# Sums over keys of the stick-breaking heads as products with the high and the low part of the softplus, and rotation of q and k with priority on VectorE

## The chip, the cores and the metric

The kernel runs on one core of one Trainium2 chip. The metric is the device time of one execution in microseconds (us). TensorE multiplies matrices into PSUM, VectorE and ScalarE work element by element, GpSimd does small work beside them, and SyncE issues most DMA transfers.

## The reference

Two blocks follow each other, for 256 positions of width 1024, all in float32. The first block has two layers; its first layer is the one that matters here. Its attention has 16 heads of 64 values each: eight stick-breaking heads and eight block-attention heads whose q and k are rotated by position first.

```
z   = q k^T / 8                                  (stick-breaking heads)
log_1mb = where(key < query, log_sigmoid(-z), 0)
after   = reverse cumulative sum over keys of log_1mb, without the key itself
a   = where(key < query, exp(log_sigmoid(z) + after), 0);   out = a v
q, k of the other eight heads: [x1 cos - x2 sin, x2 cos + x1 sin], then a causal softmax
```

Then come the projection of all heads, the gated feed-forward layers, a retention layer, and the second block of two layers.

## The kernel before

The kernel is one straight program. Weights are streamed from HBM as 1 MB tiles `raw`. ScalarE casts each to a high part `whi` (line 350, type float32r, which TensorE multiplies in one pass) and VectorE subtracts that to get a low part `wlo` (line 351). A product of two float32 matrices is then three float32r products: high by high, high by low, low by high (`mm3`; below, one group is these three products of 512 columns). Plain float32 operands are multiplied too, in two instructions each in the trace. Small float32 products and all transposes go that way.

TensorE's order is the order in which the Python program emits its instructions. A virtual clock `now` grows by a given cost per product (the last but two arguments of `mm`), and jobs (Python generators) are put into a heap with due times. Whenever a group is emitted, jobs that are due emit their part: `yield 9.42` (`D_SB`) means that the job goes on 9.42 virtual microseconds later. The orders of the other engines are written by a scheduler at build time, by a priority that is the program's order. `with self.first():` raises the priority of the instructions in it by 250 places. All orders are fixed when the kernel runs: an engine waits in its queue for whatever its next instruction needs.

In the first layer, after the first projection, each of the eight stick-breaking heads is one job (`sb_job`, line 649). Its first part multiplies k by q into a PSUM bank (256 + 128 columns; two 128-wide key blocks, the second one meeting only the second half of the queries). ScalarE then makes `e` = ln(1 + exp(-|z|)) in three passes (lines 663 to 665), and VectorE makes `sp` = max(z, 0) + e, the softplus, and masks it (lines 666, 668). Its second part, due 9.42 later, adds the sums over keys to the same bank as products of `sp` with the constant matrices `ntri` (minus one on and below the diagonal) and `nones` (all minus one), both kept in the tile `sq`. These are three float32 products of 256, 128 and 128 columns. ScalarE takes the exponential into `aT` (line 673), and VectorE masks it (line 674). `e` has three buffers (tag "sbe") and `sp` three (tag "sm").

Beside these jobs runs the projection of q and k of the other eight heads (`gemm_col`, blocks b = 1 for q, b = 2 for k, each for two halves t of the positions, eight groups each). When a half is done, its job (`epi`, line 857) rotates it on VectorE in four instructions (`rotary`, lines 616 to 619) into a tile `rows`, and 5.49 virtual microseconds later (`D_ROT0`) TensorE transposes `rows` in four instructions (line 284, from `trs`) and ScalarE copies them to `qT` or `kT` (line 865). Rotations below are counted in this order: first and second (q), third and fourth (k). The tag "rows" has four buffers of 512 columns. Also on VectorE, in the background, run the products of a vector with weights that make the modulation rows (`acc`, line 575) of three such rows in this layer; each ends in a split (`acch` line 491, `accl` line 492) that TensorE then uses.

Of the kernel before, what the change touches and what calls it, by code (L numbers as in the profile page):

```python
# [10 lines left out]
F32 = mybir.dt.float32  # L11
F32R = mybir.dt.float32r
AF = mybir.ActivationFunctionType
ALU = mybir.AluOpType
# [232 lines left out]
class Kern:  # L247
# [407 lines left out]
    def sb_job(self, q, k, aT):  # L655
        V, A = self.V, self.A
        qT, kT = q(), k()
        ps = self.bank()
        self.mm(ps[:, 0:256], kT[:, 0:128], qT, True, True, 0.432, True)
        self.mm(ps[:, 256:384], kT[:, 128:256], qT[:, 128:256], False, True, 0.216, True)  # L660
        e = self.ph.tile([128, 384], F32, tag="sbe", bufs=3, name=self.nm("sbe"))
        sp = self.ph.tile([128, 384], F32, tag="sm", bufs=self.smb, name=self.nm("sbs"))
        A.activation(e, ps[:, :384], AF.Abs)
        A.activation(e, e, AF.Exp, scale=-1.0)
        A.activation(e, e, AF.Ln, bias=1.0)
        V.scalar_tensor_tensor(sp, ps[:, :384], 0.0, e, ALU.max, ALU.add)
        d2 = lambda x: x.rearrange("p (j n) -> p j n", n=128)[:, 0:3:2]
        V.tensor_tensor(d2(sp), d2(sp), self.strict, ALU.mult)
        yield D_SB
        self.mm(ps[:, 0:256], self.ntri, sp[:, 0:256], False, True, 0.432, True)  # L670
        self.mm(ps[:, 128:256], self.nones, sp[:, 256:384], False, True, 0.216, True)
        self.mm(ps[:, 256:384], self.ntri, sp[:, 256:384], False, True, 0.216, True)
        A.activation(aT, ps[:, :384].rearrange("p (j n) -> p j n", n=128), AF.Exp)
        V.scalar_tensor_tensor(aT[:, 0:3:2], aT[:, 0:3:2], BIG, self.strict, ALU.min, ALU.mult)
        yield 2.5


    def startup(self, p):


        nc, V, A = self.nc, self.V, self.A
# [4 lines left out]
        nc.scalar.dma_start(cc, a["c"])  # L686
        self.ident = b.tile([128, 128], F32, name="ident")
        nc.scalar.dma_start(self.ident, a["k_sq"][:, 0:128])
        sq = p.tile([128, 256], F32, name="sq")
        nc.scalar.dma_start(sq, a["k_sq"][:, 128:384])  # L690
        self.ntri, self.nones = sq[:, 0:128], sq[:, 128:256]
        self.ones = p.tile([128, 128], F32, name="ones")
        V.memset(self.ones, 1.0)
        self.ones_r = p.tile([128, 128], F32R, name="ones_r")
# [67 lines left out]
        ps = [[self.bank() for _ in range(3)] for _ in range(2)]  # L762
        lst, lsv = chunks_of(D, QKV0)[0], chunks_of(D, QKV_BLOCKS)[0]
        w = {"w": {}, "v": {}}
# [58 lines left out]
    def layer0(self, lp):  # L823
        nc, V, A = self.nc, self.V, self.A
        with self.pool("l0") as p:
# [5 lines left out]
            rope = p.tile([128, 2, 3, 32], F32, name="rope64")  # L831
# [26 lines left out]
            def epi(b, t, _, ps):  # L858
                if b == 3:
                    A.copy(v[1][:, t], ps)  # L860
                    return
                rows = self.wk.tile([128, 512], F32, tag="rows", bufs=4, name=self.nm("rows"))
                self.rotary(rows, ps, rope, t, 8, 32)
                yield D_ROT0
                A.copy((qT if b == 1 else kT)[1][:, :, t * 128:t * 128 + 128], self.trs(rows, 4))

# [22 lines left out]
            for pr in range(4):  # L889

                avj[pr] = self.spawn(av(pr, [sj[i] for i in range(8)]), 1.0)
            qkj = self.gemm_col(h, "w_qkv", ch[1:3], epi, 1)
            for hd in range(8, 16):
                sj[hd] = self.spawn(score(hd, qkj), 0.5 + (hd - 8) * SP_MB)
            vj = self.gemm_col(h, "w_qkv", ch[3:4], epi, 3)
            for pr in range(4, 8):
                avj[pr] = self.spawn(av(pr, vj + [sj[i] for i in range(8, 16)]), 1.0)
# [655 lines left out]
```

## Time and profile before

| | us |
|---|---|
| median of 3 runs | 1475.32 (1473.52 to 1475.45) |
| the profiled execution: time | 1474.96 |
| the profiled execution: span of the trace | 1473.0 |
| TensorE busy in it | 1448.8 |
| VectorE busy | 1046.3 |
| ScalarE busy | 813.6 |
| GpSimd busy | 106.4 |

The span runs from the first to the last instruction that the trace holds; the profiled execution's own time is 1.96 us longer. In the rows, PE is TensorE, PEld its weight load, DVE VectorE, ACT ScalarE, POOL GpSimd. A matmul's duration is its own from start to end and overlaps the next one's; what a product costs is read from one start to the next. An engine's idle time before an instruction stands in square brackets, with what ended it. "PEclk" is the granted clock of TensorE as a share of full speed: 1.00 is 2.4 GHz, 0.50 is 1.2 GHz.

### The profile page before, as it was taken

The numbers are of one execution on the slowest core, as the hardware profiler recorded it, in microseconds if no ns is written. First come the engines' busy times: TensorE is split into PE (matmuls) and PEld (weight loads), VectorE is DVE, ScalarE is ACT, GpSimd is POOL, SyncE is SP. The second block draws the span as 40 slices with busy tenths as digits, with TensorE's granted clock in tenths as the row PEclk, the third lists the DMA queues.
The fourth block names the chain that finished last, engine by engine and source line by source line (L and its number), as shares of the span: only waits on it lengthen the run. The fifth ranks groups of instructions, "written<-read, shape, count | busy, mean of one in ns | idle before, by whom it ended". The sixth has DMA issues, their size and how long they took to land.

```text
span 1473.0 us, 19815 instructions
## 1 busy us (share of the span) xinstructions
PE 1448.8 (98%) x7476; PEld 1185.7 (80%) x7476; DVE 1046.3 (71%) x1675; ACT 813.6 (55%) x1365; POOL 106.4 (7%) x88
## 2 busy tenths in 40 slices
PE   8999999999999999999999999999999999999998
PEld 6776788887887888888878888888888888888887
DVE  5688898956988848966378756565666866666664
ACT  4657556643544535655356755666445675566651
POOL 0000000000001000000012012110000201221000
PEclk9999999999999999999999999999999999999999
DMA  9757587765776646755435455455535545555452
GB/s 380 280 201 271 199 315 287 286 207 184 284 272 243 235 165 233 297 185 197 165 123 194 166 184 210 162 177 172 193 143 190 188 147 206 195 188 189 158 175 82
DMA packets 53091, 306.64 MB, mean 208 GB/s; under 512 B 7674, under 2 KB 12154, under 8 KB 20100
## 3 DMA queue, kind: packets, MB, share of 16 engines
q1 hardware_dynamic: 51988, 304.87, 57.8%
q8 instruction: 59, 0.97, 0.3%
q10 hardware_dynamic: 1008, 0.50, 0.1%
q14 instruction: 36, 0.29, 0.1%
HBM read 301.16 MB, written 1.05 MB: 205 GB/s over the span
## 4 chain that ended last, share of the span: by engine, by line
PE 88%; DVE 5%; ACT 2%; DMA 2%; POOL 1%; issue 1%; ACTq 0%; DVEq 0%; POOLq 0%
PE p L280 84%; PE p L284 4%; DVE wlo L351 2%; ACT whi L350 1%; DMA raw<-in_w_in_dram 1%; POOL qss L487 1%; POOL ss L519 0%; DMA as<-in_ada_s_dram 0%; DVE junk L527 0%; DMA sq<-in_k_sq_dram 0%; DVE res L554 0%; DMA raw<-in_w_ao_dram 0%; DVE acc L575 0%; DVE x L555 0%; ACT sm L636 0%
## 5 line engine op out<-in xcount | busy, mean ns | idle before, releaser
L280 PE MATMUL p<-whi,hT 128*128 128x512 f32 (+1 forms) x2240 | 748.1, 401 | 4.9 <-DVE hT L492 2.7
L351 DVE TENSOR_TENSOR wlo<-raw,whi 128x1024 fp32r<-128x1024 f32 x450 | 538.2, 1215 | 147.9 <-ACT whi L350 143.9
L350 ACT CAST whi<-raw 128x1024 fp32r<-128x1024 f32 x450 | 461.8, 1045 | 242.7 <-PE p L280 189.4
L280 PEld LDWEIGHTS p<-whi,hT 128*128 128x128 f32 x2240 | 422.8, 189 | 99.7 <-issue 7.3
L280 PE MATMUL p<-wlo,hT 128*128 128x512 f32 (+1 forms) x1120 | 437.6, 391 | 0.0
L280 PEld LDWEIGHTS p<-wlo,hT 128*128 128x128 f32 x1120 | 212.1, 189 | 39.2 <-issue 1.7
L280 PE MATMUL p<-hT,whi 128*128 128x512 f32 x576 | 199.2, 398 | 0.0
L280 PE MATMUL p<-hT,wlo 128*128 128x256 f32 x576 | 149.9, 281 | 0.0
L280 PEld LDWEIGHTS p<-hT,whi 128*128 128x128 f32 x576 | 103.8, 188 | 19.6
L280 PEld LDWEIGHTS p<-hT,wlo 128*128 128x128 f32 x576 | 108.7, 189 | 6.6
L575 DVE SCALAR_TENSOR_TENSOR acc<-raw,csc,acc 128x1024 f32<-128x1024 f32 x80 | 102.2, 1277 | 3.5 <-DMA raw<-in_ada_w_dram 3.2
L487 POOL TENSOR_TENSOR dss<-dss,mh 128x8 f32<-128x8 f32 (+3 forms) x36 | 56.1, 1557 | 318.2 <-DVE dss L486 318.2
L280 PE MATMUL p<-whi,al 128*128 128x512 f32 x176 | 69.5, 395 | 0.0
L280 PE MATMUL p<-wlo,ah 128*128 128x512 f32 x176 | 69.5, 395 | 0.0
L280 PE MATMUL p<-whi,ah 128*128 128x512 f32 x176 | 69.5, 395 | 0.0
L1410 DVE TENSOR_TENSOR rows<-p,dss 128x512 f32<-128x512 f32 (+3 forms) x36 | 18.5, 514 | 46.2 <-POOL dss L487 46.2
L962 ACT COPY fT<-p 128x256 f32<-128x256 f32 x72 | 26.2, 370 | 45.2 <-PE p L280 45.2
L519 POOL TENSOR_TENSOR ss<-ss,mh 128x1 f32<-128x1 f32 x14 | 13.4, 960 | 471.2 <-DVE ss L518 471.2
L280 PE MATMUL p<-whi,s 128*128 128x512 f32 x128 | 41.3, 397 | 0.0
L280 PEld LDWEIGHTS p<-wlo,ah 128*128 128x128 f32 x176 | 33.0, 187 | 8.1
L280 PEld LDWEIGHTS p<-whi,al 128*128 128x128 f32 x176 | 33.0, 187 | 8.0
L280 PEld LDWEIGHTS p<-whi,ah 128*128 128x128 f32 x176 | 33.0, 187 | 8.0
(262 smaller groups left out, 1621.1 us busy)
## 6 DMA issues: line engine op xcount, KB each, us to landing
raw<-in_w_in_dram SPq DMA_DIRECT2D x84, 1024.0 KB, 4.9
raw<-in_w_gu_dram SPq DMA_DIRECT2D x44, 1024.0 KB, 5.2
raw<-in_ada_w_dram SPq DMA_DIRECT2D x40, 1024.0 KB, 5.3
raw<-in_w_ret_dram SPq DMA_DIRECT2D x24, 1024.0 KB, 4.9
raw<-in_w_dn_dram SPq DMA_DIRECT2D x22, 1024.0 KB, 4.9
raw<-in_w_qkv_dram SPq DMA_DIRECT2D x11, 1024.0 KB, 5.7
as<-in_ada_s_dram SPq DMA_DIRECT2D x16, 512.0 KB, 10.0
raw<-in_w_ro_dram SPq DMA_DIRECT2D x8, 1024.0 KB, 6.1
```

Source lines behind the costliest of these rows:

```text
L280: self.T.matmul(out, lhsT=lhsT, rhs=rhs, start=first, stop=last, skip_group_check=skip)
L284: self.T.transpose(out, in_, self.ident)
L350: for ins in (self.A.copy(hi[:, :m * n], src), self.V.tensor_tensor(lo[:, :m * n], src, hi[:, :m * n].bitcast(F32), ALU.subtract)):
L351: self.V.tensor_tensor(lo[:, :m * n], src, hi[:, :m * n].bitcast(F32), ALU.subtract)):
L487: self.G.tensor_tensor(ss, ss, self.mh[:, :n], ALU.pow)
L519: self.G.tensor_tensor(ss[:, 0:1], ss[:, 0:1], self.mh[:, 0:1], ALU.pow)
L575: self.V.scalar_tensor_tensor(acc, r[:, j * D:j * D + D], self.sc[:, k:k + 1], acc, ALU.mult, ALU.add)
L962: A.copy(f, ps[:, 256:512])
L1410: V.tensor_tensor(d3(rows[:, :nu * 128]), d3(src), ss[:, :2 * nu, None].to_broadcast([128, 2 * nu, 64]), ALU.mult)
```

## The change

In the stick-breaking job, `e` and `sp` move to buffers of the tag "rows" (four, shared with the rotated tiles). Two new tiles take their old buffers: `hi`, a float32r copy of `sp` made by ScalarE, and `lo` = `sp` - `hi`, made by GpSimd. The constants are cast once, at the start, to a float32r tile `sqr` by VectorE, and the tile `sq` moves to a buffer of the tag "rtmp". The three float32 products become six float32r products, three with `hi` and three with `lo`; the virtual costs become 0.12 and 0.067. The due times 9.42 and 5.49 stay. In the job of the projection, the four rotation instructions stand inside `with self.first()`.

```diff
         ps = self.bank()
         self.mm(ps[:, 0:256], kT[:, 0:128], qT, True, True, 0.432, True)
         self.mm(ps[:, 256:384], kT[:, 128:256], qT[:, 128:256], False, True, 0.216, True)
-        e = self.ph.tile([128, 384], F32, tag="sbe", bufs=3, name=self.nm("sbe"))
-        sp = self.ph.tile([128, 384], F32, tag="sm", bufs=self.smb, name=self.nm("sbs"))
+        e, sp = (self.wk.tile([128, 512], F32, tag="rows", bufs=4, name=self.nm(n))[:, 0:384] for n in ("sbe", "sbs"))
...
         V.tensor_tensor(d2(sp), d2(sp), self.strict, ALU.mult)
+
+        hi = self.ph.tile([128, 384], F32R, tag="sbe", bufs=3, name=self.nm("sbh"))
+        lo = self.ph.tile([128, 384], F32R, tag="sm", bufs=self.smb, name=self.nm("sbl"))
+        A.copy(hi, sp)
+        self.G.tensor_tensor(lo, sp, hi.bitcast(F32), ALU.subtract)
         yield D_SB
-        self.mm(ps[:, 0:256], self.ntri, sp[:, 0:256], False, True, 0.432, True)
-        self.mm(ps[:, 128:256], self.nones, sp[:, 256:384], False, True, 0.216, True)
-        self.mm(ps[:, 256:384], self.ntri, sp[:, 256:384], False, True, 0.216, True)
+        for w in (hi, lo):
+            self.mm(ps[:, 0:256], self.ntri, w[:, 0:256], False, False, 0.12, True)
+            self.mm(ps[:, 256:384], self.ntri, w[:, 256:384], False, w is lo, 0.067, True)
+            self.mm(ps[:, 128:256], self.nones, w[:, 256:384], False, w is lo, 0.067, True)
         A.activation(aT, ps[:, :384].rearrange("p (j n) -> p j n", n=128), AF.Exp)
...
-        sq = p.tile([128, 256], F32, name="sq")
+        sq = self.wk.tile([128, 256], F32, tag="rtmp", name="sq")
         nc.scalar.dma_start(sq, a["k_sq"][:, 128:384])
-        self.ntri, self.nones = sq[:, 0:128], sq[:, 128:256]
+        sqr = p.tile([128, 256], F32R, name="sqr")
+        V.tensor_copy(sqr, sq)
+        self.ntri, self.nones = sqr[:, 0:128], sqr[:, 128:256]
...
                 rows = self.wk.tile([128, 512], F32, tag="rows", bufs=4, name=self.nm("rows"))
-                self.rotary(rows, ps, rope, t, 8, 32)
+                with self.first():
+                    self.rotary(rows, ps, rope, t, 8, 32)
                 yield D_ROT0
                 A.copy((qT if b == 1 else kT)[1][:, :, t * 128:t * 128 + 128], self.trs(rows, 4))
```

## Rows read from the trace of the kernel before

**Rows 1.** The page, part 1: engine, busy us, share of the span, instructions.
```profile
PE   1448.8 (98%) x7476; PEld 1185.7 (80%) x7476; DVE 1046.3 (71%) x1675; ACT 813.6 (55%) x1365; POOL 106.4 (7%) x88
```

**Rows 2.** Waits of PE, 0 to 200 us: us in total, times, longest.
```profile
PE p L284 <- DVE rows L619: 3.7, 2, 3.4
```

**Rows 3.** Timeline of PE, 62 to 125 us: start, us, instruction, [idle before].
```profile
77.33 0.60 PE L284 MATMUL p<-ident,rows 128*128 128x128 f32 x4
77.68 0.48 PE L280 MATMUL p<-whi,hT 128*128 128x512 f32 x1
...
79.63 2.90 PE L280 MATMUL p<-sbs,sq 128*128 128x256 f32 x18
...
84.98 1.04 PE L280 MATMUL p<-sbs,sq 128*128 128x256 f32 x6
85.78 0.48 PE L280 MATMUL p<-whi,hT 128*128 128x512 f32 x1
...
87.94 1.04 PE L280 MATMUL p<-sbs,sq 128*128 128x256 f32 x6
...
94.62 1.09 PE L284 MATMUL p<-ident,rows 128*128 128x128 f32 x4 [3.38 <-DVE rows L619]
...
99.35 1.56 PE L280 MATMUL p<-sbs,sq 128*128 128x256 f32 x6
100.66 0.47 PE L280 MATMUL p<-whi,hT 128*128 128x512 f32 x1
```

**Rows 4.** Timeline of DVE, 62 to 125 us.
```profile
79.43 0.68 DVE L616 TENSOR_TENSOR rows<-p,rope 128x512 f32<-128x512 f32 x1
80.03 1.28 DVE L575 SCALAR_TENSOR_TENSOR acc<-raw,csc,acc 128x1024 f32<-128x1024 f32 x1
81.22 1.10 DVE L666 SCALAR_TENSOR_TENSOR sbs<-p,sbe 128x384 f32<-128x384 f32 x2
...
90.74 0.42 DVE L617 TENSOR_TENSOR rt<-p,rope 128x256 f32<-128x256 f32 x1
...
93.79 0.68 DVE L619 TENSOR_TENSOR rows<-rows,rt 128x512 f32<-128x512 f32 x1
```

**Rows 5.** Stretches of 1 us: busy of PE, PEld, DVE, ACT, POOL; PEclk; DMA share; GB/s.
```profile
99.00:100.00 1.00, 1.00 (x4) 0.81 (x3) 0.97 (x3) 0.00 (x0) 0.00 (x0) 0.50 0.59 250
```

**Rows 6.** Timeline of PE, 205 to 216 us: float32r products of 256 columns.
```profile
206.15 0.40 PE L280 MATMUL p<-hT,wlo 128*128 128x256 f32 x2
206.38 0.63 PE L280 MATMUL p<-hT,whi 128*128 128x512 f32 x2
```

**Rows 7.** Instructions on the tile sbs: count, duration ns min/median/max, first and last start.
```profile
L280 PEld LDWEIGHTS p<-sbs,sq x48: 186/192/337, 79.6 to 100.5; 128*128 128x128 f32 x48
```

**Rows 8.** Instructions on the tile sbe.
```profile
L663 ACT ACTIVATE sbe<-p x8: 473/487/496, 69.3 to 83.4; 128x384 f32<-128x384 f32 x8
```

**Rows 9.** Groups of GpSimd, shapes apart: count, busy us, mean ns, idle before.
```profile
L487 POOL TENSOR_TENSOR dss<-dss,mh 128x8 f32<-128x8 f32 x12 | 25.1, 2092 | 188.6 <-DVE dss L486 188.6
L566 POOL MEMSET acc<- 128x1024 f32 x10 | 9.6, 956 | 329.0 <-DVE accl L492 218.6 <-DMA raw<-in_ada_w_dram 88.2 <-issue 21.9
```

**Rows 10.** Timeline of POOL, 155 to 170 us.
```profile
160.14 0.55 POOL L519 TENSOR_TENSOR ss<-ss,mh 128x1 f32<-128x1 f32 x1 [11.22 <-DVE ss L518]
167.14 1.46 POOL L519 TENSOR_TENSOR ss<-ss,mh 128x1 f32<-128x1 f32 x1 [6.45 <-DVE ss L518]
```

**Rows 11.** Timeline of DVE, 95 to 170 us.
```profile
98.31 0.69 DVE L616 TENSOR_TENSOR rows<-p,rope 128x512 f32<-128x512 f32 x1 [1.69 <-PE p L280]
...
101.47 0.42 DVE L674 SCALAR_TENSOR_TENSOR aT<-aT,strict 128x256 f32<-128x256 f32 x1 [1.08 <-ACT aT L673]
102.72 1.23 DVE L351 TENSOR_TENSOR wlo<-raw,whi 128x1024 fp32r<-128x1024 f32 x1 [0.83 <-ACT whi L350]
...
166.99 1.21 DVE L351 TENSOR_TENSOR wlo<-raw,whi 128x1024 fp32r<-128x1024 f32 x1
```

**Rows 12.** DMA issues: line's tiles, queue, count, KB each, us to landing.
```profile
sq<-in_k_sq_dram ACTq DMA_DIRECT2D x1, 128.0 KB, 6.6
```

## The prediction

> **What bounds the kernel now.** I read the page's shares first: TensorE is busy 1448.8 of 1473.0 us [rows 1], so a change counts if it takes time from TensorE's own work or from its waits. Next the waits of TensorE, to see where its 24 idle us lie: in the first 200 us the largest is the transposes of a rotated tile waiting for VectorE, twice, 3.7 in all, the longest 3.4 [rows 2]. TensorE's timeline places the long one: it stands idle for 3.38 before 94.62 [rows 3]. VectorE's timeline says why: the second rotation starts at 79.43, and its second instruction comes at 90.74, its last at 93.79, with `acc` and other work of earlier places in the program between them [rows 4]. The data was there; the order kept it back. Last the granted clock: at 99 to 100 it is 0.50 [rows 5], the 1.2 GHz level, after that idle stretch. So the wait is paid twice, once as idle time and once as slow products behind it.
>
> **The change part by part.** The sum is made against the profiled execution, 1474.96 us.
>
> *Rotation first.* The four instructions cost VectorE the same (0.68 + 0.42 + 0.42 + 0.68 = 2.2) [rows 4], but follow each other: 79.43 + 2.2 = 81.6, in place of about 94.4. The transposes that need them came at 91.24 in TensorE's order (94.62 less the wait). By the virtual costs in the code they also move forward: the first head's sums now advance the clock by 0.51 and not 0.86, so the projection's job is spawned before the second head's sums and not after the fourth's, and its transposes stand behind the fifth head's and not the seventh's. I put them at about 87, five us after 81.6. So the 3.38 goes, and with it the 0.3 of the fourth rotation [rows 2]: 3.7.
>
> *The clock.* From 94.62 to 100.66 TensorE took 6.04 for four transposes, nine products of 512 columns (three groups) and one head's sums [rows 3]. At full clock the same cost 0.35 (77.33 to 77.68), 2.16 (85.78 to 87.94) and 0.80 (84.98 to 85.78), in all 3.3. Without the idle stretch 2.7 goes too.
>
> *The sums as six one-pass products.* Before, at full clock: 2.9 for the first three heads and 0.80 for each of the other five [rows 3], 6.9 in all. After, each head has two products of 256 columns and four of 128. The 256 are shown: two in 0.23, or 0.12 each [rows 6]. A one-pass 128 isn't shown. From below it is a quarter of a 512 product, 0.23 / 4 = 0.06; from above a weight load that nothing hides, 0.19 [rows 7]; nearest is a transpose, which also loads 128 columns and streams 128, 0.35 / 4 = 0.09 [rows 3]. With that a head costs 0.24 + 0.36 = 0.60, eight cost 4.8, and 2.1 goes. The ends: 0.48 a head, gain 3.1; 1.0 a head, loss 1.1.
>
> *hi and lo.* Between `sp` and the products two steps are added. `hi` is a ScalarE pass over 128x384, 0.49 as the pass before it [rows 8]. `lo` on GpSimd has no row: from below 0.49 (no faster than ScalarE's pass), from above 2.1, the longest group of GpSimd in the trace [rows 9]; I take 1.0, nearest to its only wide instruction, 0.96 for 1024 columns written [rows 9]. What may come on top is a hindrance by VectorE: an instruction of GpSimd on one column took 0.55 alone and 1.46 where it started 0.15 after a `wlo` of VectorE [rows 10, 11]. That is 0.9 more, and VectorE works without a gap there (79.43, 80.03, 81.22 start as the one before ends [rows 4]). So `lo` is ready 0.5 + 1.0 + 0.9 = 2.4 after `sp`.
>
> Which of this reaches TensorE? `hi` and `lo` have the three buffers that `e` and `sp` had, so the fourth head's can't be written until the first head's sums are done, at about 80.2 by the new costs. Behind its `hi` in ScalarE's queue stand the exponentials and weight casts, behind its `lo` in GpSimd's only further `lo`s and the clearing of `acc`. Its sums come at about 83 in the new order (after one group, two heads and the last head's scores), so 2.4 after 80.2 is just met. The second and third heads' are due at 81 and 81.6; there `e` and `sp` have four shared buffers, one of them kept by the rotated tile until its transposes, and VectorE takes the third head's softplus only when the first `lo` has let go of a buffer. From the fifth head on two or more groups (0.7 each) stand between heads. I take one full chain as uncovered, 2.4, in that dense stretch; the ends are 0 and the slower rival below.
>
> In sentences of its own: the Trainium skill, SBUF — State Buffer, section "Who interferes with whom", says that a VectorE instruction with two SBUF inputs and a GpSimd instruction that reads SBUF exclude each other for the whole instruction. The pair of 0.55 and 1.46 agrees. By that rule VectorE too would stand still during each `lo`, up to 8 us, an estimate, in a stretch without gaps; what that does to TensorE is the slower rival.
>
> *At no cost.* The cast of the constants is one VectorE pass of 0.42 (as L617 over 128x256 [rows 4]) at the start. It is hidden if it comes behind the first norm's work; if it stands ahead of that in the queue, that work waits for the transfer of `sq`, which takes 6.6 to land [rows 12]. I take 0 and keep a us of it in the range. The masks and the exponential are unchanged, and no DMA is added.
>
> Sum: 3.7 + 2.7 + 2.1 - 2.4 = 6.1, so 1468.9 for the profiled execution. The median shown is 0.36 above that one, and I forecast 1469.2. Its own range: with no new wait and the cheap products 3.4 less, 1465.8; with two uncovered chains 2.4 more, 1471.6.
>
> **The rivals.**
>
> *Given back later.* VectorE and not TensorE sets the pace behind the stall. For it: its idle time just there is 1.69 + 1.08 + 0.83 = 3.6 [rows 11], caused by TensorE's lateness; if the `acc` and `wlo` work of this layer is the bound, TensorE can't get further ahead than that. Against: weights are prepared several tiles ahead, and further idle gaps of VectorE follow. Time: 3.6 gained, less 2.4, is 1.2: 1474.1.
>
> *The rotation stays late.* The tile `rows` now competes with `e` and `sp` for four buffers, so the rotation with its priority still waits for a buffer. Then only 2.1 - 2.4 is left, or 1475.6, the same. For it: all four are taken at about 78. Against: the tile of the first rotation is free after 77.68 [rows 3], and the priority also takes buffers first.
>
> *Slower: `lo` late for head after head.* This is the exclusion of GpSimd and VectorE as a mechanism of this kernel: in the stretch in which VectorE runs two-input instructions without a gap, each `lo` waits for one (0.9) and holds the next up (1.0), and with buffers freed only by `lo`, the heads queue. If seven heads (second to eighth) each show 2.4, that is 16.8 in place of 2.4: 1469.2 + 14.4 = 1483.6. It decides from the fourth uncovered head: 8.5 of gains / 2.4 = 3.5. For it: VectorE's back-to-back queue at 79 to 82 [rows 4]. Against: the groups between the later heads, and that the softplus can run ahead: the fourth's and fifth's came together at 81.22 [rows 4], the fifth's products only at 84.98 [rows 3].
>
> **How the numbers follow.** The forecast has 0.55, given back later 0.18, the rotation late 0.12, the slower rival 0.15. A measurement of this kernel can tell about 0.2%, 2.95 us, from no change: faster is below 1472.4, slower above 1478.3. Faster: 0.55 and half of "given back", 0.09, is 0.64. Same: 0.09, the rotation's 0.12 and 0.01 from a mild form of the slower rival, 0.22. Slower: 0.14. The range goes from the forecast's own low end, a little further for a cheaper start, 1465, to 1476.5, which takes in the first two rivals and leaves out the slower one.
>
> **What would show it.** The transposes of the second rotation without a wait, and the granted clock at 1.00 from 90 to 101. Starts of a head's six products 0.6 apart from first to next work, not 0.8. Waits of TensorE on `lo`: about 2.4 in all; if four or more heads wait for it, the slower rival is right. The lead at the first feed-forward layer: if TensorE is ahead by 6 at 100 us and by 1 at 165, it was given back. A GpSimd subtraction well above 1.0, or the fourth rotation still late, would make single terms wrong.

## The result, and the profile after

The changed kernel takes 1495.76 us (median of 4 runs, 1494.14 to 1498.09), the kernel before 1474.49 in the runs beside it: a ratio of 1.0144, 95% interval 1.0131 to 1.0156. It is slower by 21 us. The forecast was 1469.2 with a range of 1465.0 to 1476.5; the time lies outside the range and on the other side. In the profiled executions the span grew from 1473.0 to 1492.1, by 19.1; that is what the rows below account for. Line numbers of the changed kernel are shifted: its softplus is L665 and L667, `hi` L671, `lo` L672, `aT` L678 and L679, the copy of `qT` and `kT` L873.

The page of the changed kernel, part 1, answers to [rows 1]: TensorE has 7.3 us more of busy time for products that cost less, a sign of the lower clock, and 11.8 us more without work.

```profile
PE 1456.1 (98%) x7476; PEld 1192.5 (80%) x7476; DVE 1052.2 (71%) x1676; ACT 819.9 (55%) x1373; POOL 118.4 (8%) x96
```

TensorE's waits in the changed kernel, 0 to 200 us (us in total, times, longest) answer to [rows 2].

```profile
PE p L284 <- DVE rows L619: 6.2, 1, 6.2
PE p L280 <- DVE accl L492: 4.6, 1, 4.6
PE p L280 <- ACT kT L873: 4.0, 1, 4.0
```

One rotation is waited for, where two were before, and for longer. Its place shows that it is another one. TensorE's timeline of the changed kernel, for [rows 3]:

```profile
67.84 2.06 PE L280 MATMUL p<-qT,kT 64*128 64x256 f32 x16 [0.35 <-ACT qT L859]
...
83.19 1.11 PE L284 MATMUL p<-ident,rows 128*128 128x128 f32 x4 [6.15 <-DVE rows L619]
...
98.68 0.45 PE L280 MATMUL p<-sbh,sqr 128*128 128x256 f32 x3
98.97 0.51 PE L280 MATMUL p<-sbl,sqr 128*128 128x256 f32 x3
99.31 0.45 PE L280 MATMUL p<-whi,hT 128*128 128x512 f32 x1
...
100.76 0.60 PE L284 MATMUL p<-ident,rows 128*128 128x128 f32 x4
...
121.99 2.50 PE L280 MATMUL p<-kT,qT 64*128 64x256 f32 x10 [3.99 <-ACT kT L873]
```

The transposes at 83.19 are those of the *first* rotation, which stood at 77.33 without a wait before [rows 3]. The second rotation's, at 100.76, wait for nothing, as was meant; by the run "no priority" below they wait for nothing without the priority too, so late is TensorE. VectorE's timeline of the changed kernel, for [rows 4], says why the first one is late:

```profile
72.14 0.42 DVE L667 TENSOR_TENSOR sbs<-sbs,strict 128x256 f32<-128x256 f32 x1
...
72.94 1.28 DVE L575 SCALAR_TENSOR_TENSOR acc<-raw,csc,acc 128x1024 f32<-128x1024 f32 x1
74.14 1.25 DVE L667 TENSOR_TENSOR sbs<-sbs,strict 128x256 f32<-128x256 f32 x1
75.31 3.16 DVE L351 TENSOR_TENSOR wlo<-raw,whi 128x1024 fp32r<-128x1024 f32 x2
...
80.39 0.55 DVE L665 SCALAR_TENSOR_TENSOR sbs<-p,sbe 128x384 f32<-128x384 f32 x1
80.86 0.68 DVE L616 TENSOR_TENSOR rows<-p,rope 128x512 f32<-128x512 f32 x1
...
82.45 0.68 DVE L619 TENSOR_TENSOR rows<-rows,rt 128x512 f32<-128x512 f32 x1
```

VectorE's rows of the kernel before, which [rows 4] doesn't have, are these: the first L616, and a pair of `wlo` and two splits that are needed below.

```profile
66.67 0.69 DVE L616 TENSOR_TENSOR rows<-p,rope 128x512 f32<-128x512 f32 x1 [3.57 <-PE p L284]
...
75.96 2.35 DVE L351 TENSOR_TENSOR wlo<-raw,whi 128x1024 fp32r<-128x1024 f32 x2
...
122.84 1.23 DVE L492 TENSOR_TENSOR accl<-acc,acch 128x1024 fp32r<-128x1024 f32 x1 [0.43 <-ACT acch L491]
...
146.68 1.23 DVE L492 TENSOR_TENSOR accl<-acc,acch 128x1024 fp32r<-128x1024 f32 x1 [1.11 <-ACT acch L491]
```

Before, the first L616 started at 66.67, after 3.57 without work, as soon as TensorE let it. Now it comes at 80.86, right behind the softplus of the fourth head: `e` and `sp` of the heads ahead of it in the program pass through the four buffers of the tag "rows" first. The stretches of 1 us of the changed kernel, for [rows 5], give the price behind the wait: TensorE is at 0.50, the 1.2 GHz level, from the wait on until past 98. In these 15.1 us, 0.8 of them idle, it does some 7.5 us of work, so 7.5 are lost.

```profile
84.00:85.00 1.00, 1.00 (x5) 0.76 (x3) 1.00 (x2) 1.00 (x3) 0.00 (x0) 0.50 0.95 393
...
97.00:98.00 1.00, 1.00 (x4) 0.81 (x3) 1.00 (x2) 0.68 (x3) 1.00 (x1) 0.50 0.00 0
...
99.00:100.00 1.00, 1.00 (x8) 0.92 (x7) 1.00 (x4) 0.49 (x1) 0.00 (x0) 1.00 0.78 205
```

From the first scores of the stick-breaking heads to the causal scores TensorE took 45.5 us before (68.29 to 113.79, in its rows below) and takes 54.2 (67.84 to 121.99).

```profile
68.29 2.06 PE L280 MATMUL p<-qT,kT 64*128 64x256 f32 x16 [0.35 <-ACT qT L852]
...
113.79 1.46 PE L280 MATMUL p<-kT,qT 64*128 64x256 f32 x10 [0.55 <-ACT kT L865]
```

The sum: wait 6.2, half clock 7.5, the wait for `kT` 3.99 in place of 0.55, so 3.4 more; less the second rotation's and the fourth's wait and the clock behind them, 6.4 by the forecast's terms. That is 10.7, and 8.7 was measured; the 2.0 between is about what the cheaper products were to save (2.1). The wait for `kT` comes from ScalarE's queue: the copy stands behind two casts of weights, and these start 7.9 us after their tile was issued (111.61 to 119.46), where before it was 5.0 (106.30 to 111.26).

```profile
119.46 1.99 ACT L350 CAST whi<-raw 128x1024 fp32r<-128x1024 f32 x2 [2.04 <-DMA raw<-in_w_ao_dram]
```

It does not simply follow from the late rotation: in the run "changed, rows first" below the first rotation is waited for just as long, and `kT` for 0.3.

The rest is lost further on. The third of the modulation rows is split by VectorE at 146.68 in the trace before, and at 171.19 now; the second one at 122.84 before and at 141.93 now. VectorE's rows of the changed kernel:

```profile
141.93 1.22 DVE L492 TENSOR_TENSOR accl<-acc,acch 128x1024 fp32r<-128x1024 f32 x1
171.19 1.22 DVE L492 TENSOR_TENSOR accl<-acc,acch 128x1024 fp32r<-128x1024 f32 x1
```

TensorE waits for it, and runs at half clock again until 176.8 (2.2 of work lost):

```profile
172.46 0.79 PE L280 MATMUL p<-accl,ones_r 128*128 128x512 f32 x1 [4.57 <-DVE accl L492]
```

The transposes of the first norm of the feed-forward layer start at 180.82, before at 163.18: 17.6 later, of which 8.2 were lost by the causal scores. Of the other 9.4, the wait for the split is 5.0 (4.57, and 0.45 for its high part), the half clock behind it 2.2, and the half clock behind the wait for `kT` (122.2 to 125.6) 1.7; 0.5 is not accounted for. Behind that point little happens (span less that start: 1311.3, before 1309.8).

### The profile page after: what moved, and what is told of

The parts are those of the page before. It is cut to its first block, busy times and chain, and to the rows that moved or that the text cites. A ratio compares the mean times of both kernels' runs of the same rounds, so it can differ in the third digit from the quotient of the medians.

```text
span 1492.1 us, 19833 instructions
## 1 busy us (share of the span) xinstructions
PE 1456.1 (98%) x7476; PEld 1192.5 (80%) x7476; DVE 1052.2 (71%) x1676; ACT 819.9 (55%) x1373; POOL 118.4 (8%) x96
## 4 chain that ended last, share of the span: by engine, by line
PE 88%; DVE 6%; DMA 2%; issue 1%; ACT 1%; POOL 1%; DVEq 0%; ACTq 0%; POOLq 0%; SPq 0%
PE p L280 84%; PE p L284 4%; DVE wlo L351 2%; DMA raw<-in_w_in_dram 1%; ACT whi L350 1%; DVE acc L575 1%; DMA raw<-in_w_ao_dram 1%; DMA raw<-in_ada_w_dram 0%; POOL qss L487 0%; DVE junk L527 0%; DVE res L554 0%; POOL ss L519 0%; DVE x L555 0%; POOL kss L1338 0%; DVE sbs L667 0%
```

## The experiments

For each run the table has four readings of its trace: when the first stick-breaking scores start, the length of the stage from there to the causal scores, the start of the first norm's transposes, and the rest of the profiled execution's span from there to the end; then the ratio of its times to those of the kernel before on the same chip, with its interval. "Own buffer" gives the rotated tile a buffer of another tag, "lo on VectorE" moves the subtraction there from GpSimd, "rows first" raises the instructions of the first layer's modulation rows, "splits first" only their splits.

| | stage from | stage | norm at | rest | ratio |
|---|---|---|---|---|---|
| before | 68.29 | 45.5 | 163.18 | 1309.8 | 1 |
| changed | 67.84 | 54.2 | 180.82 | 1311.3 | 1.0144 [1.0131, 1.0156] |
| changed, own buffer | 70.79 | 44.3 | 167.40 | 1310.6 | 1.0010 [0.9995, 1.0024] |
| changed, lo on VectorE | 71.31 | 50.2 | 172.66 | 1310.2 | 1.0043 [1.0025, 1.0061] |
| before with priority alone | 70.33 | 38.4 | 171.92 | 1311.5 | 1.0052 [1.0034, 1.0070] |
| changed, no priority | 69.10 | 55.0 | 183.09 | 1313.1 | 1.0140 [1.0110, 1.0170] |
| own buffer, lo on VectorE | 67.73 | 44.3 | 168.98 | 1313.5 | 1.0048 [1.0031, 1.0065] |
| priority alone, rows first | 69.42 | 40.7 | 162.18 | 1309.6 | 1.0010 [0.9996, 1.0024] |
| changed, rows first | 67.71 | 52.2 | 175.41 | 1310.0 | 1.0086 [1.0070, 1.0102] |
| own buffer, lo on VectorE, rows first | 67.66 | 50.5 | 169.32 | 1310.9 | 1.0056 [1.0040, 1.0073] |
| priority, high part only | 69.81 | 39.0 | 169.31 | 1310.4 | 1.0093 [1.0065, 1.0120] |
| own buffer, no priority | 67.85 | 47.7 | 165.38 | 1309.7 | 1.0046 [1.0030, 1.0061] |
| softplus in own buffers | 67.82 | 49.3 | 168.23 | 1313.0 | 1.0087 [1.0065, 1.0110] |
| priority alone, splits first | 69.22 | 38.4 | 162.06 | 1310.3 | 1.0009 [0.9996, 1.0023] |

The rest stays between 1309.6 and 1313.5: most of what these kernels differ by has happened by the first norm. The stage starts between 67.66 and 71.31, and "norm at" holds this too. The start goes with the granted clock of the first 40 us: the six traces that have 1.00 in the first and the second 20 us start the stage at 67.66 to 67.85, the two with 0.91 and 0.92 or 0.92 and 0.90 (own buffer, `lo` on VectorE) at 70.79 and 71.31. What puts the clock there in one trace and not in another is not shown. The length of the stage and "norm at" don't follow each other, and that is the second half of the answer.

**Own buffer for the rotated tile.** Is it the shared buffers?

```diff
-                rows = self.wk.tile([128, 512], F32, tag="rows", bufs=4, name=self.nm("rows"))
+                rows = self.wk.tile([128, D], F32, tag="xn", name=self.nm("rows"))[:, 0:512]
```

> The changed kernel, but the rotated tile of the eight rotated heads stands in a buffer of the tag xn (two buffers, idle in this stretch) and not in one of the four of the tag rows that e and sp use. TensorE's order is the same as in the changed kernel. Theory A (the shared buffers hold the first rotation back until four softplus heads have passed through them, which stops TensorE for 6.15 us and leaves some 7 us of half clock): the first rotation starts near 66 us, the wait of 6.15 before its transposes is gone, and the time falls by at least 13 us, to 1482 or below. If the later waits (4.0 on kT, 4.6 on the low part of a modulation row) only follow from that lateness, it falls to about 1470; if they come from the new order, it stays near 1481. Theory B (the longer chain hi, lo and GpSimd's port): TensorE waits on hi or lo in its place, time above 1488. Theory C (the raised priority itself spoils VectorE's order): above 1488.

1477.78, so 1.0010 in place of 1.0144, with TensorE's order unchanged. The wait of 6.15 is gone and the first rotation runs at 68.73, before the first scores. VectorE's row, and TensorE's waits, 62 to 182 us, which hold what is left:

```profile
68.73 0.69 DVE L616 TENSOR_TENSOR rows<-p,rope 128x512 f32<-128x512 f32 x1 [3.13 <-PE p L280]
```

```profile
PE p L280 <- POOL sbl L672: 2.0, 3, 0.9
PE p L280 <- DVE rt L618: 1.7, 1, 1.7
PE p L280 <- ACT kT L873: 1.6, 1, 1.6
PE p L284 <- ACT sm L640: 1.3, 2, 0.9
```

With the rotation on time, TensorE does meet `lo` too early, for 2.0 in three heads. The 1.7 is a wait for the second rotation's L618, the last of its instructions that reads the product, and about 3.4 us at half clock follow it. No gain over the kernel before is left.

**`lo` on VectorE.** Is it GpSimd?

```diff
-        self.G.tensor_tensor(lo, sp, hi.bitcast(F32), ALU.subtract)
+        V.tensor_tensor(lo, sp, hi.bitcast(F32), ALU.subtract)
```

> The changed kernel, but lo is subtracted on VectorE and not on GpSimd. Buffers and priority as changed. Theory A: the first rotation still waits for a buffer; 1488 to 1498. Theory B (GpSimd's subtraction of 1.0 to 1.8 us and its port hold the heads and their buffers): the wait before the first transposes shrinks below 3 us and the time falls under 1482. Theory C: no change.

1482.45, between the ranges of A and B, and the wait for the first rotation is still 4.4. `lo` takes 0.55 there, and the first rotation starts 11.1 after the first scores (82.42 - 71.31) in place of 13.0, still behind the heads. So GpSimd is a part of that delay, 1.9 by this run. Most of the 13.3 us that this run is faster than the changed kernel lies later: its waits for `kT` (0.9 in place of 4.0) and for the third modulation row (none in place of 4.6) are shorter too. Whether that is GpSimd's doing or the newly written order's is not shown.

**Priority alone.** What is the other half of the change worth by itself?

```diff
-                self.rotary(rows, ps, rope, t, 8, 32)
+                with self.first():
+                    self.rotary(rows, ps, rope, t, 8, 32)
```

> The kernel before with only the raised priority of the rotation. Theories A and B: the second rotation's instructions follow each other, TensorE's wait of 3.38 and its half clock go, and the time falls by about 6 us, to 1468 to 1470. Theory C: slower than before.

No rotation is waited for, and the clock is full from 80 to 120: the stage is 7.1 shorter (45.5 to 38.4). And yet the kernel is slower, 1483.14, so the times of theories A and B are missed and C's sign is right. TensorE's timeline of this run, 150 to 170 us:

```profile
162.31 0.80 PE L280 MATMUL p<-acch,ones_r 128*128 128x512 f32 x1 [9.52 <-ACT acch L491]
163.57 0.79 PE L280 MATMUL p<-accl,ones_r 128*128 128x512 f32 x1 [0.46 <-DVE accl L492]
```

The third modulation row, split at 146.68 before, is split at 162.29 here. The rows are one chain on VectorE: a single accumulator `acc`, which the next row may use only when the split of the last has read it.

**No priority.** The changed kernel, with the diff just shown taken back.

> The changed kernel without the raised priority. Theory A: the first rotation waits for a buffer just as long or longer, so 1490 or more. Theory C: the time falls back to 1480 or below. Theory B: 1485 to 1495.

1496.43: no different from the changed kernel. The first rotation is waited for 7.1, and TensorE is so late by it that the second one is not waited for even without priority, and the fourth for 0.2.

**Own buffer and `lo` on VectorE.** The first two diffs together.

> The changed kernel with the rotated tile in its own buffer (as in e1) and lo on VectorE (as in e2). Buffers account for the first wait, GpSimd for the 2.0 us of waits on lo that e1 still has. Theory A with GpSimd as the second term: the time falls 2 to 6 us below e1, to 1472 to 1476 beside a kernel before of 1475. Rival (VectorE is the bound and each lo on it costs as much as it saves): the same as e1 or slower, 1477 or more.

Missed: 1482.12, in the rival's range. The stage is as long as with GpSimd, with waits of 2.7 for `hi` and 1.5 for `lo`, and at the first norm TensorE stands 6.5 behind VectorE.

**Priority alone, rows first.** Can the given-back time be kept by raising the rows?

```diff
+                with self.first() if l == 0 and v in (2, 3, 4) else ExitStack():
-                self.V.scalar_tensor_tensor(acc, ...)
+                    self.V.scalar_tensor_tensor(acc, ...)
...
+        with self.first() if l == 0 and v in (2, 3, 4) else ExitStack():
-        self.split(hi, lo, acc)
+            self.split(hi, lo, acc)
```

> The kernel before with the raised priority of the rotation, as e3, and the same raised priority for the products acc and the split of the three modulation rows of the first layer. Theory D (the gain of about 7 us that e3 has at 108 us is given back because the third modulation row comes late, a wait of 9.5 and its half clock): that wait goes and the time falls to 1466 to 1472. Rival (the row is late because of its transfers or because VectorE has too much work, whatever its order): the wait stays above 4 us, time above 1478.

The wait of 9.5 is gone, and the ratio falls from 1.0052 to 1.0010, some 6 us. With the run "priority alone, splits first" below, this shows that the late third row was what made the priority alone slower. But the result is the time of the kernel before and no less, a partial miss.

**Changed, rows first.** The same two edits on the changed kernel.

> The changed kernel with the raised priority for the modulation rows of the first layer. Theory A and D: the first wait of about 6 us and its half clock stay, the wait of 4.6 on the third row goes with its half clock, so 5 to 9 us less than the changed kernel: 1486 to 1491. Rival (the late row only follows from the late start): no change, 1494 to 1497.

1487.47, as expected: the wait for the late third row is gone, the first rotation's (6.3) stays.

**Own buffer, `lo` on VectorE, rows first.**

> e5 with the raised priority for the modulation rows. If all three causes are right and independent, this has the rotation on time, the cheap sums and the rows on time: 1466 to 1472, faster than the kernel before. Rival (VectorE is full and every priority displaces something that TensorE waits for): 1474 or more.

Missed: 1482.81. `hi` is now waited for 4.7 in two heads (longest 2.9), and the clock is 0.74 from 80 to 100. VectorE is busy for 19.4 of these 20 us. That what is raised here pushes the heads back is argued from this; no run shows it.

**Priority, high part only.** The kernel before with the priority, the softplus written as float32r, three one-pass products a head with the constants cast as in the changed kernel; the low part is left out of the computation. The diff is shortened.

```diff
-        sp = self.ph.tile([128, 384], F32, ...)
+        sp = self.ph.tile([128, 384], F32R, ...)
...
+        self.mm(ps[:, 0:256], self.ntri, sp[:, 0:256], False, False, 0.24, True)
+        self.mm(ps[:, 256:384], self.ntri, sp[:, 256:384], False, True, 0.134, True)
+        self.mm(ps[:, 128:256], self.nones, sp[:, 256:384], False, True, 0.134, True)
```

> The kernel before with the priority, and the softplus written by VectorE straight as one float32r tile: three one-pass products a head in place of three float32 ones; the low part is left out of the computation. The virtual costs are those of the six products in sum, so TensorE's order is the changed kernel's. Theory: with own buffers and without the steps hi and lo between softplus and products, no head waits for its softplus; the stretch from the end of the first q and k transposes to the causal scores is 33 to 38 us (priority alone had 38.4, the changed kernel with an own buffer for the rotated tile 44.3). What is gained may be given back at the third modulation row, as with priority alone: 1474 to 1483. Rival: TensorE's new order, not the steps hi and lo, makes that stretch longer: 43 to 46 us here too, and 1476 to 1480.

The stage is 39.0, just above the 33 to 38 of the theory, against 44.3 with `hi` and `lo` and an own buffer. Three products a head fewer are worth 8 x 0.3 = 2.4; the other 2.9 no run splits up. The own buffer's waits for `lo` (2.0) and for the second rotation (1.7) are gone here, but one head waits 3.0 for its softplus, and the stage is not shorter than with priority alone (38.4). The total, 1482.87, is at the upper end of the range, and VectorE's rows of this run show why:

```profile
154.71 1.22 DVE L492 TENSOR_TENSOR accl<-acc,acch 128x1024 fp32r<-128x1024 f32 x1 [1.11 <-ACT acch L491]
...
158.25 2.35 DVE L351 TENSOR_TENSOR wlo<-raw,whi 128x1024 fp32r<-128x1024 f32 x2
...
165.97 1.28 DVE L591 SCALAR_TENSOR_TENSOR bc<-p,bc 128x512 f32<-128x512 f32 x2
167.16 1.40 DVE L527 SCALAR_TENSOR_TENSOR junk<-x,ss,bc 128x512 f32<-128x512 f32 x2
```

The third row is split at 154.71 and TensorE multiplies it at 156.18. But in VectorE's order weights and the other half of the projection stand ahead of the norm's instructions, which come at 165.97 and 167.16 (the norm's L527 before: 160.73). The edit names none of these instructions; the order was written anew for the whole kernel at build time.

**Own buffer, no priority.** The first experiment without `with self.first()`.

> The changed kernel with an own buffer for the rotated tile (the form that measured 1477.8) and without the priority. Theory: the priority is worth the wait of the second rotation and the half clock behind it, also in this form: the second rotation's transposes wait 2 to 4 us, 1481 to 1486. Rival: VectorE's load sets the pace of this stage in any order, the priority only moves the lateness: 1475 to 1479.

1477.67, the rival's number: the second rotation waits 0.95 and not 2 to 4. TensorE lost its time elsewhere, at `aT` of a head:

```profile
PE p L280 <- ACT aT L678: 5.7, 2, 3.7
...
PE p L284 <- DVE rows L619: 1.0, 1, 1.0
```

Its ratio (1.0046) is above that of the first experiment (1.0010), which the rival did not expect; the two were compared with the kernel before on different chips, so the difference of some 5 us stays open.

**Softplus in own buffers.** The other way to end the sharing: `e` and `sp` side by side in one tile with two buffers, the rotated tile alone in "rows".

```diff
-        e, sp = (self.wk.tile([128, 512], F32, tag="rows", bufs=4, name=self.nm(n))[:, 0:384] for n in ("sbe", "sbs"))
+        es = self.wk.tile([128, D], F32, tag="xn", name=self.nm("sbe"))
+        e, sp = es[:, 0:384], es[:, 512:896]
```

> The changed kernel, but e and sp lie side by side in one tile of two buffers of their own (tag xn), and the rotated tile alone stays in the tag rows. Theory: what made the changed kernel late was that the first rotation shared its buffers with e and sp: its wait (6.2 us) and the half clock behind it go, first rotation between 66 and 70 us, 1474 to 1481. Rival: the number of buffers isn't it; the heads with two pairs of e and sp are as late as with shared ones and the first rotation stays late: 1488 to 1498.

The mechanism is confirmed: the first rotation starts at 66.2, and TensorE's rows of this run have its transposes at 76.85 without a wait. The time is between the two ranges, 1484.1. Two pairs are too few: ScalarE waits for GpSimd's `lo` to let go of one five times between 73 and 97, 6.8 us in all, and TensorE waits behind that:

```profile
76.85 0.60 PE L284 MATMUL p<-ident,rows 128*128 128x128 f32 x4
...
80.48 0.92 PE L280 MATMUL p<-qT,kT 64*128 64x256 f32 x4 [2.33 <-ACT qT L874]
...
91.60 0.56 PE L280 MATMUL p<-sbh,sqr 128*128 128x256 f32 x3 [1.57 <-ACT sbh L672]
93.57 0.90 PE L280 MATMUL p<-sbl,sqr 128*128 128x256 f32 x3 [1.41 <-POOL sbl L673]
```

**Priority alone, splits first.** Only the second of the two edits of "rows first".

> The kernel before with the priority, and of the modulation rows of the first layer only the splits (acch and accl) raised too, not the products acc. Theory: the third row came late because its split stood behind other work in VectorE's and ScalarE's queues: PE's wait of 9.5 us for acch at 162 us shrinks to under 2, and 1468 to 1475. Rival: the products acc themselves were late (their weights and their place), the split's rank changes nothing: the wait stays at 7 to 10 us, 1480 to 1485.

1474.52: the wait for the third row is gone (its split comes at 149.56). The causal scores are reached after 38.4, and the first norm only 1.1 us earlier than before. The time between is seen in TensorE's waits of this run, 110 to 142 us,

```profile
PE p L284 <- ACT sm L641: 2.1, 2, 1.4
PE p L280 <- ACT aT L643: 1.2, 1, 1.2
```

and in its stretch 125 to 135, whose clock is 0.56:

```profile
125.00:135.00 10.00, 8.02 (x22) 5.05 (x23) 7.82 (x20) 9.47 (x31) 0.40 (x1) 0.56 0.24 78
```

From the causal scores to the first product of the heads' projection it takes 20.5 us (107.62 to 128.11) where the kernel before took 18.55 (113.79 to 132.34), and from there to the norm 33.95 where it took 30.84. Of 7.1 gained, 5.1 go back in the softmax and behind it; 0.9 is a later start of the whole stage. This version does not beat the kernel before (0.9996 to 1.0023), and none of the others does.

## Why the prediction was wrong

**Rotation first, and the rival "the rotation stays late".** Here it failed. The terms 3.7 and 2.7 were right for the second rotation: with priority alone the stage is 7.1 shorter, against 6.4. But I looked at that rotation alone. The change also put the first one, which waited for nothing, into one ring of buffers with `e` and `sp` of four heads. I had named the shared buffers and dismissed them with "the tile of the first rotation is free after 77.68, and the priority also takes buffers first". The first clause is about the buffer that the first rotation leaves, not the one that it needs; the second is not so here: the rotation had the priority and still came behind the heads that stand ahead of it in the program. And the rival's price, 1475.6, held only the gain that would be missed. A rotation that moves from 66.67 to 80.86 is a new wait, 6.2, with a new stretch at half clock, 7.5. These two are 13.7. With an own buffer they go, and 18 us in all, but not one for one: the stage is 9.9 shorter (54.2 to 44.3), since new waits for `lo` and for the second rotation come in, and 6.5 more is saved between the causal scores and the norm, where the wait for the third row goes too. That second part is not the ring's alone: this wait also goes with `lo` on VectorE and with the rows first, where the first rotation is still late.

**The clock.** The mechanism was right, and so was the size for the wait that goes; it was not applied to the one that comes. The length of the slow stretch is not in proportion to the wait: 15.1 us behind 6.15, 3.4 behind 3.99, 4.3 behind 4.57, and 6.0 behind 3.38 before.

**Six products.** 0.60 a head was forecast; the rows give 99.31 - 98.68 = 0.63, and the same 0.62 to 0.64 at 101.90 and 104.65, so 1.9 and not 2.1 for eight heads at full clock.

**hi and lo.** 0.5 and 1.0 plus up to 0.9 were forecast; `hi` takes 0.51, `lo` 1.00 to 1.83. As the changed kernel stands, no head waits for them, since TensorE is behind. Where the rotation is on time, the uncovered part is 2.0 (own buffer) to 5.2 (own buffer, `lo` on VectorE, rows first). The 2.4 of the sum lies at the lower end of this, and it eats what the products save.

**Given back later.** This rival had 0.18, and it holds for the part of the change that works. Its reason was not VectorE's load as I had it, but VectorE's order: each edit re-orders the background work, and the chain of modulation rows had some 9 us of slack (TensorE multiplies at 156.65 what VectorE's split ends at 147.9). Priority alone brought TensorE there at 152.8 and the split to 162.3; raising the rows got this back, and what stayed was spent in the softmax.

**Slower: `lo` late head after head.** The sign was right, the mechanism in part: `lo` and VectorE do hold each other up (last section), which makes the first rotation 1.9 later. But TensorE meets the queue of heads at that rotation; among the changed kernel's waits there is none for `lo`.

**At no cost.** The cast of the constants is not the cause: the first scores come at 67.84, before at 68.29. But the clock of the first 20 us was 1.00 and 0.91 in these two traces. At 0.91 the changed kernel without priority has them at 69.10, so 0.8 for the cast and the order around it is not excluded, within the us that the range kept.

What stays open: whether the split's rank alone or the whole new order around it moves the third row, since each edit rewrites all orders. A form with `e` and `sp` in four buffers of their own was not tried.

## What to carry to other kernels

When a change lets new tiles share a ring of buffers, go through every tile that takes from that ring, in program order, those that waited for nothing first; a priority moves an instruction in its queue, it does not let its tile pass another's. Where the orders of the engines are fixed at build time, don't end the sum at the stage that is edited: name the next result that all orders meet at (here the third modulation row and the first norm), and how much slack it has in the trace before. Here 7 us gained in one stage became a loss because the new order moved that result by 15.6 (2.0 of it a later start of the stage).

## What the runs showed of the hardware that was not expected

In this trace GpSimd and VectorE hold each other up for about a whole instruction, and only for some of VectorE's. The prediction's sum has this for GpSimd; on VectorE's side it stands only in the slower rival. GpSimd's timeline of the changed kernel:

```profile
73.36 1.74 POOL L672 TENSOR_TENSOR sbl<-sbs,sbh 128x384 fp32r<-128x384 f32 x1 [62.96 <-ACT sbh L671]
...
81.09 1.00 POOL L672 TENSOR_TENSOR sbl<-sbs,sbh 128x384 fp32r<-128x384 f32 x1 [3.70 <-ACT sbh L671]
...
96.75 1.83 POOL L672 TENSOR_TENSOR sbl<-sbs,sbh 128x384 fp32r<-128x384 f32 x1 [1.65 <-ACT sbh L671]
```

The subtraction at 81.09 runs beside the rotation's L616 to L618, which read one operand from PSUM: 1.00, and L616 keeps its 0.68. The one at 73.36 begins while `acc` (two inputs from SBUF) runs until 74.22, ends 0.9 later, and VectorE's L667 at 74.14, also with two, takes 1.25 in place of 0.42; the two `wlo` behind it take 3.16 beside the next `lo`, 2.35 before. So each of the first two subtractions cost VectorE about 0.8, in the very chain that the first rotation stood behind; that the rotation starts 1.9 earlier with `lo` on VectorE fits the two. The Trainium skill, SBUF — State Buffer, section "Who interferes with whom", states that an instruction of VectorE with at most one SBUF input, outside its two-port modes, does not contend with GpSimd, that one with two contends with a GpSimd instruction that reads SBUF, and that the shared ports are an exclusive lock. These rows agree.
